# Weight sums of block products made in DRAM by accumulating transfers, five plain pairs, and block products kept in the program's order

## The chip, the cores and the metric

The kernel runs on one core of a Trainium2 chip. Its time is the device time of one execution in microseconds. TensorE (PE) multiplies matrices out of SBUF into PSUM, VectorE (DVE) and ScalarE (ACT) work elementwise, GpSimd (POOL) computes nothing here, and SyncE (SP) issues nearly all transfers. Each engine takes its instructions in a fixed order, which a planner sets when the program is built: it goes by the order in which the program was written, by estimated costs, and by when operands are due, and it may move an instruction ahead of an earlier one on its engine.

## What is computed

One step of a small backbone of two layers on 512 latent and 128 context tokens, D = 1024. Layer 0 has a bidirectional scan (SSD) as token mixer, layer 1 differential attention. After each mixer comes a ConvGLU network:

```python
def conv_ffn(h, up_w, conv_w, conv_b, down_w):
    u = dwconv(h @ up_w, conv_w, conv_b)      # up_w 1024 x 5632, width-3 filter along the tokens
    a, v = jnp.split(u, 2, axis=-1)
    return (jax.nn.silu(a) * v) @ down_w      # down_w 2816 x 1024
```

Every sublayer is preceded by an RMS norm with shift, scale and gate that are computed from a conditioning vector by a 1024 x 6144 matrix per layer (the "modulation").

## The kernel before

Activations lie transposed, channels on partitions, the 640 tokens along the free axis. For near-fp32 products each operand is split in two fp32r parts, `hi` (ScalarE copies with rounding) and `lo` (VectorE subtracts), and a product is three matmuls: hi·hi, hi·lo, lo·hi. One step of a plain product is a matmul of 256 and one of 384 columns.

The stages in order are SSD, first network, attention, second network. A network has 22 pairs of hidden tiles (a tile of `a`, a tile of `v`, 128 channels each) and goes through them in three groups; after each group the down projection adds what the group's tiles give (`project_out`, the last time `project_last`). A weight unit is a tile of 128 x 1024 floats (512 KB). SyncE loads it into one of four buffers (`prefetch`, L301), `cast` (L309) splits it into one of five pairs of hi and lo buffers, and `nextw` (L332) hands it over, loads up to three units ahead and casts one ahead. Up projections use PSUM tiles of two banks, of which there are three.

In the second network pairs 0 to 3 (`STD = 4`) are plain. From pair 4 on, the up projection works on blocks: the contraction (1024) is cut in two halves of 512, the tokens in two halves of 320, and the pair has two rows of weight blocks, x1 x2 for `a` and y1 y2 for `v`. A Strassen-Winograd scheme takes 7 block products, where the plain form would need 8; each has 4 contraction steps of 3 matmuls, so 12 matmuls of 320 columns. It needs sums of blocks of the activations (`sums`, L61, made once, while the first plain pairs run, by a task that `hook` advances; VectorE adds, ScalarE and VectorE split) and sums of blocks of the weights, per pair four (s1 to s4). These are made by VectorE in `stage` (L119), as `s[0] = y1 + y2`, `s[1] = s[0] - x1`, `s[2] = x1 - y1`, `s[3] = x2 - s[1]`, each 128 x 512, and every one of the seven blocks is split by itself, except that x1 and x2 share one wide split in every second pair. `plan` (L102) writes the order of the products by hand, `stage` works up to `LOOK = 7` products ahead of it.

A pair's products go 1, 2, (3 of the pair before), 6, (4 of the pair before), 5, 7 (`pair`, L175). Products 1, 6, 7 and 4 go into one PSUM half tile: 6, 7 and 4 add to what is there, and before each of them ScalarE copies the state so far out (`ua`, `uv`), since it is part of a result. VectorE adds products 2, 3 and 5 to these copies. Product 3 adds to 5's bank. Three half tiles serve a pair and six alternate. Then `epilogue` filters `a` and `v` along the tokens (ScalarE and VectorE), takes the SiLU, multiplies, and splits the result for the down projection. Products 3 and 4 of the last pair of a group come in the down projection behind its first tile (`between`, L210).

During the first network a task, `mod_rest` (L703), computes the modulation of layer 1 on VectorE: 48 columns, each from a 512 KB load on SP's queue (`mw`, two buffers) and two reductions (L725).

Of the kernel before, what the change touches and what calls it, by code (L numbers as in the profile page):

```python
# [41 lines left out]
STD = 4  # L42
HT = T // 2
LOOK = 7
# [5 lines left out]
class Blocks:  # L50


    def __init__(self, st, h, epilogue, pool):
        self.st, self.h, self.epilogue, self.pool = st, h, epilogue, pool
        self.ops = {}
        self.pend = None
        self.spare = None
        self.half = None
        self.units = sorted(st.paired)

    def sums(self):  # L61
# [5 lines left out]
        for j in range(4):  # L67
# [34 lines left out]
    def plan(self, p0, p1):  # L102

        self.seq, self.done, self.at = [], 0, 0
        for p in range(p0, p1):
            prev = p > p0
            self.seq += [(1, p), (2, p)] + [(3, p - 1)] * prev + [(6, p)] + [(4, p - 1)] * prev + [(5, p), (7, p)]
        self.seq += [(0, p1 - 1), (3, p1 - 1), (4, p1 - 1)]

    def place(self):  # L110

        if self.half is None:
            hi, lo = self.st.parts()
            self.half = hi[:, 512:], lo[:, 512:]
            return hi[:, :512], lo[:, :512]
        o, self.half = self.half, None
        return o

    def stage(self, upto):  # L119

        st = self.st
        k1, k2 = slice(0, 512), slice(512, 1024)
        while self.done < min(upto, len(self.seq)):
            i, p = self.seq[self.done]
            self.done += 1
            if i == 0:
                self.half = None
                st.cast(self.units[2 * (p - STD)] + 2)
                continue
            o = self.ops.setdefault(p, {})  # L130
            if i == 1:
                u = self.units[2 * (p - STD)]
                st.prefetch(u + 1)
                x, y = st.wraw[u], st.wraw[u + 1]
                s = [self.pool.tile([P, 512], F32, tag=f"s{n}", name=f"s{n}_{p}", bufs=1) for n in range(1, 5)]
                st.tt(s[0], y[:, k1], y[:, k2], ALU.add)
                st.tt(s[1], s[0], x[:, k1], ALU.subtract)
                st.tt(s[2], x[:, k1], y[:, k1], ALU.subtract)
                o["raw"] = {1: x[:, k1], 2: x[:, k2], 4: y[:, k2], 5: s[0], 6: s[1], 7: s[2], 3: s[3]}
                if self.half is None:  # L140
                    hi, lo = st.parts()
                    st.split_w(hi, lo, x)
                    o[1], o[2] = ((hi[:, k], lo[:, k]) for k in (k1, k2))
            if i == 6:
                st.tt(o["raw"][3], o["raw"][2], o["raw"][6], ALU.subtract)
            if i not in o:
                o[i] = self.place()
                st.split_w(*o[i], o["raw"][i])

    B = {1: "11", 2: "21", 3: "22", 4: 4, 5: 1, 6: 2, 7: 3}  # L150
# [24 lines left out]
    def pair(self, p):  # L175
        st = self.st
        st.wi = self.units[2 * (p - STD)] + 2
        st.prefetch(st.wi + 1)
# [31 lines left out]
    def between(self, i, p0, p1):  # L210

        st = self.st
# [9 lines left out]
        if i == 6:  # L222
            self.stage(LOOK)


class Step:


    def __init__(self, ctx, tc, a):
# [12 lines left out]
        self.paired = set()  # L242
        self.npart = 0
# [57 lines left out]
    def prefetch(self, upto):  # L301
        while len(self.wraw) <= min(upto, len(self.units) - 1):
            u = len(self.wraw)
            ap, n = self.units[u]
            r = self.pw.tile([P, 1024], F32, tag="raw", name=f"raw{u}", bufs=RAW)
            self.nc.sync.dma_start(r[:, :n], ap)
            self.wraw[u] = r

    def cast(self, upto):  # L309
        while len(self.wcast) <= min(upto, len(self.units) - 1):  # L310
            u = len(self.wcast)
            self.prefetch(u)
            if u in self.paired:
                self.wcast[u] = None
                continue
            n = self.units[u][1]
            hi, lo = (t[:, :n] for t in self.parts())
            self.split_w(hi, lo, self.wraw[u][:, :n])
            self.wcast[u] = hi, lo

    def parts(self):
        v = self.npart
        self.npart += 1
        wp, t, b = (self.pw, "w", 3) if self.px is None or v % 5 < 3 else (self.px, "x", 2)
        return [wp.tile([P, 1024], F32R, tag=t + nm, name=f"w{nm}{v}", bufs=b) for nm in ("hi", "lo")]

    def split_w(self, hi, lo, raw):

        self.act(hi, raw, AF.Copy)
        self.tt(lo, raw, hi.bitcast(F32), ALU.subtract)  # L330
# [136 lines left out]
    def project_out(self, h, ks, g, tiles=range(KT), after=None):  # L467

        for i in tiles:
            ps = self.dense_ps("po")  # L470
            self.dense(ps, self.nextw(), ks, h)
# [231 lines left out]
    def mod_rest(self, l, t0, pool):  # L703
# [11 lines left out]
        for t in range(t0 - 1, 48):  # L715
# [8 lines left out]
            for c in range(2):  # L724
                nc.vector.tensor_tensor_reduce(w if c else junk, w, cb[:, c, :], 1.0, 0.0, ALU.mult, ALU.add,  # L725
                                               self.mod[l][:, t, c:c + 1])
                yield 2 if self.down else 7
            if t % KT == KT - 1:
# [16 lines left out]
    def ffn(self, l, h, nextnorm, pool):  # L745
# [27 lines left out]

        self.start_tiles(h)
        done = 0
        sub = SUB[l]
        blk = Blocks(self, h, epilogue, pool) if l else None
        for s, (k0, k1) in enumerate(sub):
# [3 lines left out]
            if blk and s == 0:  # L782
                blk.plan(STD, end)
# [14 lines left out]
            after = blk and (lambda i: blk.between(i, done, min(sub[s + 1][1] + 1, FT) if not last else done))  # L798
            if not last:
                self.project_out(mid, range(k0, k1), self.gate(l, 1), after=after)  # L800
            else:
                self.project_last(mid, range(k0, k1), self.gate(l, 1), nextnorm, parts="CD" if l else "AB",
                                  after=after)
# [550 lines left out]
    def weight_units(self):  # L1354
        a = self.a
        u = [(a["w_dt"], 512)]
# [3 lines left out]
        u += [(a["w_in"][j], 1024) for j in order]  # L1360
        for hf in range(2):
            u += [(a["w_so"][i, :, hf * 1024:(hf + 1) * 1024], 1024) for i in range(KT)]

        def ffn(l):
            done = 0
            out = []
            for k0, k1 in SUB[l]:
                while done < min(k1 + 1, FT):
                    if l and done >= STD:
                        self.paired |= {len(u) + len(out), len(u) + len(out) + 1}  # L1370
                    out.extend([(a["w_up"][l, done], 1024), (a["w_up"][l, FT + done], 1024)])
                    done += 1
                out.extend([(a["w_dn"][l, i, :, k0 * P:k1 * P], (k1 - k0) * P) for i in range(KT)])
# [3 lines left out]
        for hd in range(8):  # L1377
            u += [(a["w_qkv"][8 * j + hd], 1024) for j in range(3)]
# [137 lines left out]
```

## Time and profile before

| | |
|---|---|
| median of 3 runs (lowest to highest) | 1885.05 us (1882.87 to 1887.03) |
| the profiled execution | 1884.19 us |
| its span, first to last instruction | 1882.4 us |
| granted TensorE clock, mean | 0.991 |
| busy: PE, DVE, ACT, POOL | 98%, 79%, 53%, 0% |
| read from and written to HBM | 201.63 MB, 5.96 MB |

All times below are microseconds from the start of this execution's span. TensorE works on the first network from about 568 to 1038, on attention to about 1406, on the second network from then on: its first block product begins at 1465.6, its last down projection ends near 1867. "PE" rows are matmuls, "PEld" rows the loading of stationary operands, and "<-" in brackets names what ended an engine's idle time before a row. L277, L280, L283 and L286 are helpers, so rows of theirs are told apart by their tiles: `whi`, `wlo` are weight parts, `s` the four sums, `ba`, `bb`, `bc` the PSUM tiles of block products, `up` and `po` those of plain up and down projections, `T` and `h11` activation parts.

### The profile page before, as it was taken

The numbers are of one execution on the slowest core, as the hardware profiler recorded it, in microseconds if no ns is written. First come the engines' busy times: TensorE is split into PE (matmuls) and PEld (weight loads), VectorE is DVE, ScalarE is ACT, GpSimd is POOL, SyncE is SP. The second block draws the span as 40 slices with busy tenths as digits, with TensorE's granted clock in tenths as the row PEclk, the third lists the DMA queues.
The fourth block names the chain that finished last, engine by engine and source line by source line (L and its number), as shares of the span: only waits on it lengthen the run. The fifth ranks groups of instructions, "written<-read, shape, count | busy, mean of one in ns | idle before, by whom it ended". The sixth has DMA issues, their size and how long they took to land. (4 is left out here: it accounts for less than half of the span.)

```text
span 1882.4 us, 32863 instructions
## 1 busy us (share of the span) xinstructions
PE 1841.4 (98%) x13117; PEld 1727.3 (92%) x13117; DVE 1478.4 (79%) x2886; ACT 991.6 (53%) x1880; POOL 0.2 (0%) x4
## 2 busy tenths in 40 slices
PE   7999999999999999999999999999999899999997
PEld 4789899989989999999999988888899799999996
DVE  4689999999748999984455877778779885975974
ACT  2479687879336441442343565656546442643651
POOL 0000000000000000000000000000000000000000
PEclk9999999999999999999999999999999899999998
DMA  9735243446543556632222212111031131231221
GB/s 344 256 109 147 92 133 117 117 136 177 186 136 108 190 182 218 188 119 80 77 68 68 88 52 64 47 59 40 23 119 52 55 104 60 73 114 57 68 79 56
DMA packets 79521, 209.72 MB, mean 111 GB/s; under 512 B 9116, under 2 KB 15880, under 8 KB 79240
## 3 DMA queue, kind: packets, MB, share of 16 engines
q1 hardware_dynamic: 78792, 207.10, 34.7%
q8 instruction: 103, 1.69, 0.4%
q10 hardware_dynamic: 576, 0.52, 0.1%
q14 instruction: 50, 0.41, 0.1%
HBM read 201.63 MB, written 5.96 MB: 110 GB/s over the span
## 5 line engine op out<-in xcount | busy, mean ns | idle before, releaser
L277 ACT ACTIVATE whi<-raw 128x1024 fp32r<-128x1024 f32 (+4 forms) x238 | 228.3, 961 | 303.1 <-PE po L286 187.7
L283 DVE TENSOR_TENSOR wlo<-raw,whi 128x1024 fp32r<-128x1024 f32 (+4 forms) x238 | 261.9, 1102 | 79.7 <-ACT whi L277 67.8
L280 DVE SCALAR_TENSOR_TENSOR xr<-po,mod,xr 128x256 f32<-128x256 f32 (+2 forms) x231 | 89.3, 434 | 138.0 <-PE po L286 137.9
L286 PE MATMUL po<-ml,whi 128*128 128x256 f32 (+1 forms) x704 | 168.2, 310 | 0.0
L286 PE MATMUL po<-mh,whi 128*128 128x256 f32 (+1 forms) x704 | 168.0, 310 | 0.0
L286 PE MATMUL po<-mh,wlo 128*128 128x256 f32 (+1 forms) x704 | 167.8, 310 | 0.0
L286 PE MATMUL up<-h01h,wlo 128*128 128x256 f32 (+1 forms) x656 | 149.4, 308 | 0.0
L286 PE MATMUL up<-h01l,whi 128*128 128x256 f32 (+1 forms) x656 | 149.3, 308 | 0.0
L286 PE MATMUL up<-h01h,whi 128*128 128x256 f32 (+1 forms) x656 | 149.3, 308 | 0.0
L286 PEld LDWEIGHTS po<-mh,whi 128*128 128x128 f32 x704 | 128.4, 188 | 0.5 <-ACT mh L277 0.2
L286 PEld LDWEIGHTS po<-mh,wlo 128*128 128x128 f32 x704 | 128.8, 188 | 0.0
L286 PEld LDWEIGHTS po<-ml,whi 128*128 128x128 f32 x704 | 128.6, 188 | 0.1
L286 PEld LDWEIGHTS up<-h01h,wlo 128*128 128x128 f32 x656 | 119.3, 188 | 0.0
L286 PEld LDWEIGHTS up<-h01l,whi 128*128 128x128 f32 x656 | 119.3, 188 | 0.0
L286 PEld LDWEIGHTS up<-h01h,whi 128*128 128x128 f32 x656 | 119.2, 188 | 0.0
L277 ACT ACTIVATE whi<-s 128x512 fp32r<-128x512 f32 x72 | 44.5, 626 | 60.7 <-PE po L286 20.6
L277 ACT ACTIVATE mh<-cv 128x640 fp32r<-128x640 f32 x44 | 32.5, 738 | 79.3 <-DVE cv L283 79.1
L277 ACT ACTIVATE e<-sl,sm 128x640 f32<-128x640 f32 x64 | 50.4, 790 | 40.2 <-DVE sm L1225 39.8
L286 PE MATMUL z<-h00h,whi 128*128 128x256 f32 (+1 forms) x256 | 62.9, 325 | 0.0
L277 ACT ACTIVATE e<-rb,Ctok 128x128 f32<-128x128 f32 x160 | 56.4, 390 | 12.3 <-issue 10.0
L277 ACT ACTIVATE ca<-ca 128x640 f32<-128x640 f32 x44 | 32.4, 736 | 57.0 <-DVE ca L280 56.8
L286 PE MATMUL z<-h00l,whi 128*128 128x256 f32 (+1 forms) x256 | 59.8, 312 | 0.0
(558 smaller groups left out, 5154.7 us busy)
## 6 DMA issues: line engine op xcount, KB each, us to landing
raw<-in_w_up SPq DMA_DIRECT2D x88, 512.0 KB, 3.4
mw<-in_modT SPq DMA_DIRECT2D x48, 512.0 KB, 3.6
raw<-in_w_in SPq DMA_DIRECT2D x40, 512.0 KB, 5.2
rb<-rowd SPq DMA_DIRECT2D x40, 512.0 KB, 5.3
raw<-in_w_dn SPq DMA_DIRECT2D x32, 448.0 KB, 3.4
raw<-in_w_qkv SPq DMA_DIRECT2D x24, 512.0 KB, 3.4
mr<-in_mod SPq DMA_DIRECT2D x44, 256.0 KB, 5.5
raw<-in_w_so SPq DMA_DIRECT2D x16, 512.0 KB, 4.2
```

The costliest lines, as they stand in the source:

```text
L277: return self.nc.scalar.activation(out, in_, func, **k)
L280: return self.nc.vector.scalar_tensor_tensor(out, in0, s, in1, op0, op1)
L283: return self.nc.vector.tensor_tensor(out, a, b, op)
L286: return self.nc.tensor.matmul(out, lhsT, rhs, start=start, stop=stop, **k)
```

## The change

- `STD` goes from 4 to 5: pairs 0 to 4 are plain, 17 pairs work on blocks.
- The four weight sums of these 17 pairs are made in DRAM. `weight_sums` issues, on GpSimd's queue, four plain copies and four transfers that add to what lies at their destination (`accum_op`), each for up to three pairs at once and 256 KB a pair. Each waits for those whose result it uses. They are issued in six groups of nine transfers from within `mod_rest`, at columns 4, 12, 20, 28, 36 and 44; a first transfer of two floats, which reads the modulation column just made, ties the group to that time. VectorE and SP have no part in it.
- So that only additions are needed, `v`'s block row is taken with the opposite sign: the activation sums change theirs, operand 2's parts are made negated (`neg`), and the three filter taps of `v` in the block pairs are multiplied by -1 once, at the start of the second network.
- The blocks then are ordinary weight units, loaded by SP from the weights or from the sums in the order in which the products use them: one wide unit for products 1 and 2 where these fall together, otherwise two halves of 256 KB in one buffer. One `cast` splits a unit of 128 x 1024. `plan`, `place`, `stage` and their lists go, and so do the buffers s1 to s4.
- In the second network's weights the two contraction halves of a tile lie apart in DRAM (`w_blk`), so a plain unit is loaded in rows of 2 KB rather than 4.
- `nextw` casts three units ahead (`AHEAD`) for block products and the second network's down projections, and loads up to five ahead, still into four buffers.
- The first matmul of each block product is pinned behind everything that was traced on TensorE before it (`keep_in_program_order`). Other matmuls are not pinned.

```diff
-STD = 4
+STD = 5
-LOOK = 7
+AHEAD = 3
...
-            st.tt(t1, a[:, c2], a[:, c1], ALU.subtract)
-            st.tt(t2, b[:, c2], t1, ALU.subtract)
-            st.tt(t4, b[:, c1], t2, ALU.subtract)
+            st.tt(t1, a[:, c1], a[:, c2], ALU.subtract)
+            st.tt(t2, b[:, c2], t1, ALU.add)
+            st.tt(t4, t2, b[:, c1], ALU.subtract)
...
-                st.split_w(t[:, c1], t[:, c2], x)
+                st.split_w(t[:, c1], t[:, c2], x, i == 2)
...
     def finish_sums(self):
         st, h, t = self.st, self.h, self.t
-        self.stage(LOOK)
+        st.cast(st.wi + 1)
...
     def product(self, ps, i, p):
         st = self.st
-        self.at += 1
-        self.stage(self.at + LOOK)
-        wh, wl = self.ops[p].pop(i)
+        if self.half is None:
+            hi, lo = st.nextw(AHEAD)
+            wh, wl = hi[:, :512], lo[:, :512]
+            if hi.shape[1] > 512:
+                self.half = hi[:, 512:], lo[:, 512:]
+        else:
+            (wh, wl), self.half = self.half, None
...
-                st.mm(ps, a[:, c], b, not acc and j == 0 and m == 0, j == 3 and m == 2, skip_group_check=acc)
+                x = st.mm(ps, a[:, c], b, not acc and j == 0 and m == 0, j == 3 and m == 2, skip_group_check=acc)
+                if j == 0 and m == 0:
+                    st.tc.keep_in_program_order(x)
...
-    def between(self, i, p0, p1):
-
-        st = self.st
+    def between(self, i):
         if i == 0:
+            self.half = None
             self.third()
             self.fourth()
             self.half = self.spare = None
-            if p1 > p0:
-                self.plan(p0, p1)
-        if i == 4:
-            st.cast(st.wi + 2)
-            self.stage(4)
-        if i == 6:
-            self.stage(LOOK)
...
-    def nextw(self):
+    def nextw(self, ahead=1):
         u = self.wi
         self.wi += 1
-        self.prefetch(u + 3)
-        self.cast(u + 1)
+        self.prefetch(u + 2 + ahead)
+        self.cast(u + ahead)
         return self.wcast[u]
...
+            if t % 8 == 4 and t < 48:
+                n = -(-(FT - STD) // 6)
+                p0 = STD + t // 8 * n
+                if p0 < FT:
+                    self.weight_sums(p0, min(p0 + n, FT), self.mod[l][0:1, t, :])
...
+            t = cw[:, FT + STD:, 0:3]
+            nc.vector.tensor_scalar(t, t, -1.0, None, ALU.mult)
...
+            def piece(i, p):
+                if i in (1, 2, 4):
+                    return a["w_blk"][p + FT * (i == 4), int(i > 1)], 512
+                return (lambda: self.wsum[p - STD, (5, 6, 7, 3).index(i)]), 512
...
+                    if seq[n][0] == 1:
+                        out.append(up(seq[n][1])[0])
+                    else:
+                        out.append([piece(*q) for q in seq[n:n + 2]])
+                    n += 2
...
+    def weight_sums(self, p0, p1, mark):
+
+        g, w, s = self.nc.gpsimd, self.a["w_blk"], self.wsum
+        rows = lambda x: x.rearrange("n p c -> n (p c)").rearrange("n (r c) -> r n c", c=2048)
+        a1, a2, n = slice(p0, p1), slice(FT + p0, FT + p1), slice(p0 - STD, p1 - STD)
+        put = lambda i, x, **k: g.dma_start(rows(s[n, i]), rows(x), **k)
+        add = dict(accum_op=ALU.add)
+        g.dma_start(s[p0 - STD, 0, 0:1, 0:2], mark)
+        put(0, w[a2, 0])
+        put(2, w[a1, 0])
+        put(0, w[a2, 1], **add)
+        put(2, w[a2, 0], **add)
+        put(1, s[n, 0])
+        put(1, w[a1, 0], **add)
+        put(3, s[n, 1])
+        put(3, w[a1, 1], **add)
```

More of the change, by code (lines that the diff above doesn't have):

```diff
@@ L58, in __init__ @@
         self.half = None
-        self.units = sorted(st.paired)
     def sums(self):
@@ L119, in stage @@
-    def stage(self, upto):
-        st = self.st
[L122 to L143, printed above, removed]
-            if i == 6:
[L145 to L148, printed above, removed]
@@ L797, in ffn @@
                 self.drain(self.modtask)
-            after = blk and (lambda i: blk.between(i, done, min(sub[s + 1][1] + 1, FT) if not last else done))
             if not last:
-                self.project_out(mid, range(k0, k1), self.gate(l, 1), after=after)
+                self.project_out(mid, range(k0, k1), self.gate(l, 1), after=blk and blk.between)
             else:
                 self.project_last(mid, range(k0, k1), self.gate(l, 1), nextnorm, parts="CD" if l else "AB",
-                                  after=after)
+                                  after=blk and blk.between)
     def ssd_consts(self, pool):
@@ L1367, in ffn @@
             for k0, k1 in SUB[l]:
[L1368 to L1371, printed above, removed]
+                end = min(k1 + 1, FT)
+                while done < end and not (l and done >= STD):
+                    out += up(done)
                     done += 1
-                out.extend([(a["w_dn"][l, i, :, k0 * P:k1 * P], (k1 - k0) * P) for i in range(KT)])
+                seq = []
+                for p in range(done, end):
+                    prev = p > done
+                    seq += [(1, p), (2, p)] + [(3, p - 1)] * prev + [(6, p)] + [(4, p - 1)] * prev + [(5, p), (7, p)]
+                n = 0
+                while n < len(seq):
+                    if seq[n][0] == 1:
+                        out.append(up(seq[n][1])[0])
+                    else:
+                        out.append([piece(*q) for q in seq[n:n + 2]])
+                    n += 2
+                dn = down(k0, k1)
+                if seq:
+                    dn.insert(1, [piece(3, end - 1), piece(4, end - 1)])
+                done = end
+                out += dn
             return out
```

86 lines of the change are left out of this document (36 added, 50 removed).

## The prediction

> **What bounds the kernel now.** I read the page first, then the windows view by stage, the waits of the one stretch that loses time, its timeline, the groups by form, and the transfers.
>
> ```profile
> span 1882.4 us, 32863 instructions
> PE 1841.4 (98%) x13117; PEld 1727.3 (92%) x13117; DVE 1478.4 (79%) x2886; ACT 991.6 (53%) x1880; POOL 0.2 (0%) x4
> PEclk9999999999999999999999999999999899999998
> ```
>
> TensorE is busy 98% of the span, so a gain has to come from TensorE waits or from fewer TensorE cycles. The clock line shows one dip inside the program, slice 32 of 47 us each, which begins at 1459 us. The windows view cuts that place out; its columns are length, then busy time of PE, PEld, DVE, ACT, POOL, then granted clock, DMA share and GB/s.
>
> ```profile
> 575.00:700.00 125.00, 125.00 (x849) 125.00 (x848) 120.29 (x219) 66.84 (x90) 0.00 (x0) 1.00 0.53 169
> 700.00:755.00 55.00, 55.00 (x377) 55.00 (x377) 54.12 (x98) 9.26 (x10) 0.00 (x0) 1.00 0.68 215
> 1405.00:1465.00 60.00, 60.00 (x433) 59.16 (x432) 55.48 (x123) 39.77 (x68) 0.00 (x0) 1.00 0.14 45
> 1465.56:1489.80 24.24, 17.19 (x74) 14.93 (x73) 21.05 (x38) 8.27 (x15) 0.00 (x0) 0.72 0.20 66
> 1489.80:1527.20 37.40, 36.71 (x242) 35.64 (x243) 31.85 (x59) 22.85 (x39) 0.00 (x0) 1.00 0.31 89
> 1600.00:1720.00 120.00, 119.39 (x805) 1.00 0.27 82
> ```
>
> The first network (575 on) and the plain pairs of the second (1405 to 1465) leave TensorE no gap. The first 24 us of block products do: 74 matmuls at a granted clock of 0.72. After 1490 almost nothing is lost (119.39 of 120 us busy). So the change can win in one place, the start of the block products. Its waits (total us, times, longest) and parts of its timeline:
>
> ```profile
> ACT whi L277 <- PE ba L286: 9.0, 2, 6.8
> PE ba L286 <- DVE ua L283: 2.1, 1, 2.1
> PE ba L286 <- DVE wlo L283: 1.8, 1, 1.8
> PE ba L286 <- ACT ua L277: 1.7, 2, 1.2
> ```
>
> ```profile
> 1461.74 0.46 PE L286 MATMUL up<-h11h,wlo 128*128 128x256 f32 x2
> 1464.68 0.46 PE L286 MATMUL up<-h11h,whi 128*128 128x256 f32 x2
> ...
> 1469.17 0.42 PE L286 MATMUL ba<-h11h,wlo 128*128 128x320 f32 x1 [1.84 <-DVE wlo L283]
> 1471.49 0.47 PE L286 MATMUL ba<-h11h,wlo 128*128 128x320 f32 x1
> 1471.99 0.44 ACT L277 ACTIVATE ua<-ba 128x320 f32<-128x320 f32 x1 [3.25 <-PE ba L286]
> 1472.48 0.63 PE L286 MATMUL ba<-h11h,whi 128*128 128x320 f32 x1 [0.53 <-ACT ua L277]
> 1473.18 0.47 PE L286 MATMUL ba<-h11h,wlo 128*128 128x320 f32 x1
> 1475.32 0.47 PE L286 MATMUL ba<-h11l,whi 128*128 128x320 f32 x1
> 1478.36 0.31 PE L286 MATMUL bc<-h11h,whi 128*128 128x320 f32 x1
> 1479.39 0.31 PE L286 MATMUL bc<-h11l,whi 128*128 128x320 f32 x1
> ```
>
> Cadences from the starts: a plain step (one 256 and one 384 column matmul) takes (1464.68 - 1461.74)/10 = 0.294 us. A block matmul of 320 columns takes (1479.39 - 1478.36)/7 = 0.147 us, and (1475.32 - 1473.18)/8 = 0.268 us while the clock is down. VectorE is late with weight parts and sums (21.05 of 24.24 us busy, after 55.48 of 60), TensorE waits 1.84 us for one, loses its clock and computes six microseconds at little over half speed; then ScalarE and VectorE are late once more. Of the 74 matmuls two belong to the plain pair; 72 x 0.147 = 10.6 us were needed, 24.24 were taken: **13.6 us lost**, some 7 by waits and the rest by the clock.
>
> The Trainium skill, "TensorE: Matmul & The Clock Gate", section "What's actually happening", has the clock halve after an idle window of about 3.4 us. Here no single wait was that long (1.84 us, 0.47 us before it) and the clock fell all the same, so the row decides; by the rule a stall left over of 1 or 2 us would cost itself alone.
>
> **The change part by part.**
>
> *Sums and weight parts on VectorE.* Groups by form, 1465 to 1815 us:
>
> ```profile
> L283 DVE TENSOR_TENSOR wlo<-s,whi 128x512 fp32r<-128x512 f32 x72 | 48.7, 687 | 9.6 <-ACT whi L277 9.6
> L283 DVE TENSOR_TENSOR wlo<-raw,whi 128x512 fp32r<-128x512 f32 x34 | 23.1, 689 | 0.2
> L283 DVE TENSOR_TENSOR wlo<-raw,whi 128x1024 fp32r<-128x1024 f32 x14 | 17.1, 1223 | 2.6 <-ACT whi L277 2.6
> L283 DVE TENSOR_TENSOR s<-raw,s 128x512 f32<-128x512 f32 x18 | 12.4, 688 | 0.1
> L283 DVE TENSOR_TENSOR s<-raw,raw 128x512 f32<-128x512 f32 x18 | 12.4, 688 | 0.0
> L283 DVE TENSOR_TENSOR s<-s,raw 128x512 f32<-128x512 f32 x17 | 11.7, 688 | 0.1
> L283 DVE TENSOR_TENSOR s<-raw 128x512 f32<-128x512 f32 x17 | 11.7, 686 | 0.0
> L277 ACT ACTIVATE whi<-raw 128x1024 fp32r<-128x1024 f32 x14 | 14.8, 1055 | 18.2 <-PE po L286 10.7 <-PE ba L286 7.3 <-PE bb L286 0.3
> ```
>
> Four sums of 0.69 us a pair go: 72 x 0.688 = 49.5 us of VectorE. The parts are then made 1024 wide: 3.5 a pair at 1.223 = 4.3 us, against five of 0.688 and half a wide one, two halves of 0.69 in the other pairs, 4.7 us. A pair asks VectorE for 3.2 us less of the 7 x 12 x 0.147 = 12.3 us that TensorE takes for it. By itself that is hidden work, except at the start, where it is what TensorE waits for.
>
> *Five plain pairs.* Pair 4 becomes 48 x 0.294 = 14.1 us in place of 12.3: **+1.8 us** on the path. In return VectorE gets 14 us more before the first block product. The four pairs up to 1465, with the norm's tail and the activation sums, kept it busy 55.48 us, 13.9 a pair; the added pair has neither norm nor sums, only an epilogue and weight parts, and the block sums that stood in the queue at 1465 are gone, so what it is behind can be caught up. The first block unit is then an ordinary unit, cast ahead. So nearly all of the 13.6 us goes: **-13.6**, and I leave **+1.0** for what is still late (bounds 0 and 7, the waits without the clock). What is late next is an epilogue of the plain pairs, wanted only by the down projection three block pairs (37 us) on.
>
> *Products in the program's order.* Each product's first matmul is put behind all that was traced on TensorE. Where a run of blocks begins, 6 follows 1 with only product 2 between, and 7 follows 6 with only 5 between, both into a bank that ScalarE must copy first. The cover is 12 x 0.147 = 1.76 us. The chain in the timeline, from the issue of the last matmul (1471.49) to the first that may write the bank again (1472.48), takes 1.0 us with a free ScalarE, so 0.76 us is left; a wide cast in the way (1.055 us) overruns it by 0.3. Behind a waiting product stand all later ones, then their copies on ScalarE and adds on VectorE. Three runs x two places x 0.2: **+1.2 us** (bounds 0 and 6 x 0.6 = 3.7). In later pairs two products or more lie between, 3.5 us of cover: I take 0 (bounds -2, the small switches after 1490, and the second rival).
>
> *Weights by pieces.* 17 pairs ask for 119 blocks of 256 KB: 31.2 MB where 17.8 were loaded, in 10 wide and 99 half transfers where 34 were; at 0.33 us of SP each that is 25 us more over 400. 1.84 MB in 12.3 us is 149 GB/s; the windows show 215 GB/s moved at 700 to 755 with no TensorE gap. A buffer comes free four units (14 us) before its data is due and a load lands in 3.4 us. At nothing; without that cover each unit could lose up to 3.4 us.
>
> *The sums in DRAM.* 17 x 8 transfers of 0.262 MB = 35.7 MB written, 54 issues on POOL (it has 4 instructions now; nothing stands behind them). Each group starts when a modulation column (4, 12, ... 44) is done, so somewhat behind the loads of these columns, and is wanted from about 1475: from 616 on, 41 GB/s would do. They run beside these:
>
> ```profile
> raw<-in_w_up SPq DMA_DIRECT2D x88, 512.0 KB, 3.4
> mw<-in_modT SPq DMA_DIRECT2D x48, 512.0 KB, 3.6
> L718 SPq DMA_DIRECT2D mw<-in_modT x48: 327/328/328, 584.9 to 815.6; - x48
> ...
> DVE junk L725 <- DMA mw<-in_modT: 1.3, 3, 0.8
> ...
> 717.48 3.13 SPq L718 DMA_DIRECT2D mw<-in_modT  x2
> ...
> 722.35 1.22 DVE L725 CUSTOM_DVE_ANT_0 junk<-mw,cbc 128x1024 bf16<-128x1024 f32 x1
> ...
> ACT whi L277 <- PE po L286: 96.5, 21, 6.1
> ```
>
> A share of 0.68 at 215 GB/s means 316 GB/s at full use; 35.7 MB then take 113 us of all engines, 169 if the four accumulating transfers in eight read twice. Were all of it laid on the loads of 585 to 900 us, 48 of the modulation and 45 of weights (one each 7.05 us), each would land 1.8 us later. A modulation load has 722.35 - 717.48 = 4.9 us for its 3.6, so some would hold VectorE 0.5 us, and VectorE has no room there (54.12 of 55). TensorE would not feel it soon: casts wait for TensorE to free a buffer (96.5 us of such waits), not the other way. **+0.3 us** (bounds 0 and the third rival). No row has an accumulating transfer; the nearest are the plain loads, and I stay near them since only the total matters.
>
> The sign change of the filter taps is one small VectorE operation; its data are issued at 1368.8, 35 us ahead of the start of that network:
>
> ```profile
> L748 SPq DMA_DIRECT2D fcw<-in_fcw x2: 327/328/328, 535.4 to 1368.8; - x2
> ```
>
> **Sum:** -13.6 + 1.0 + 1.8 + 1.2 + 0.3 = **-9.3 us**. The profiled execution took 1884.19 us (span 1882.4 and 1.8 around it), the median of the runs is 0.86 above: 1885.05 - 9.3 = **1875.7 us**. Measurements of this kernel tell 0.2%, 3.8 us, from no change.
>
> **Rivals.** *First, half of the loss stays.* VectorE was 92% busy before the start and still is in pairs 0 to 3; if it is as late after pair 4, the 7 us of waits stay and only the clock's share goes: -6.6 + 1.8 + 1.2 + 0.3 = -3.3, 1881.8. For it: the activation sums are not made smaller. Against: 14 us of new room.
>
> *Second, slower: the order itself costs.* Now the planner puts a later product into each wait; pinned, products 6 and 7 of every pair wait for ScalarE's copy, which stands behind whatever ScalarE does. One such wait later on:
>
> ```profile
> 1646.41 0.41 PE L286 MATMUL bb<-h11h,whi 128*128 128x320 f32 x1 [0.61 <-ACT ua L277]
> ```
>
> At 0.61 us each, 34 products lose 20.7 us in place of 1.2: 1895. It decides from 10.5/34 = 0.31 us each. For it: ScalarE is in order and waits up to 6.8 us at a cast. Against: ScalarE loses 14 us of narrow casts, is busy little over half, and 3.5 us of cover beat a chain of 1.0.
>
> *Third, the sums crowd the first network.* If modulation loads take twice as long, 7.2 us, two columns need 7.2 + 2.6 = 9.8 us of a down unit of 8 x 3 x 0.294 = 7.05: VectorE falls back 22 us in eight units, and behind its gate additions TensorE has three PSUM tiles, two units or 14 us, of cover. 8 us come through: 1884; with no cover, 1898.
>
> The Trainium skill, "DMA: Bandwidth & Descriptors", section "Issuing engines are not separate DMA queues", speaks for this rival: transfers of SP and GpSimd share the same 16 engines and interleave. This trace has no transfer from POOL, so it can't show how far they slow each other.
>
> *Fourth, the sums are late* (under 41 GB/s) and TensorE waits at 1475 for them: tens of microseconds. Against it stand 650 us between the last modulation load and the first use.
>
> **Numbers.** Forecast (1869 to 1880) 0.62, first rival 0.14, second 0.12, third 0.10, fourth 0.02. Faster by over 0.2% (below 1881.3): the forecast, a third of the first and a little of the third, 0.68. Within: most of the first and half the third, 0.15. Slower: the second, fourth and the rest, 0.17. The low end is all 13.6 us and the small switches gone with nothing given back but the plain pair, 1885 - 13.6 - 2 + 1.8 = 1871, and 3 us below it for what I can't see; the high end takes the first and third rival and the beginning of the second, 1888.
>
> **What would show it.** Right: at the start of the block products, then near 1479, TensorE without gaps over 1 us and the clock at 1.00; no sums on VectorE; the first network's windows still full; waits for a copy only at the first pair of a run. Wrong: a clock under 1 there, waits of products 6 and 7 for ScalarE in every pair, idle VectorE before the modulation columns, or block products that wait for a weight transfer.

## The result and the profile after

The changed kernel takes **1936.05 us** (median of 4 runs, 1932.70 to 1938.54) beside 1885.74 us for the kernel before, measured with it (1882.87 to 1887.03): a ratio of 1.0268, 95% interval 1.0248 to 1.0288. It is 2.7% slower, where 0.5% faster was forecast. Its profiled execution has a span of 1934.0 us, 51.6 more than before.

The page of the kernel after: span, busy time, and from the 40 slices (48 us each) those of the clock and of the DMA engines.

```profile
span 1934.0 us, 32975 instructions
PE 1847.1 (96%) x13129; PEld 1731.5 (90%) x13129; DVE 1433.1 (74%) x2759; ACT 984.1 (51%) x1825; POOL 38.7 (2%) x58
...
PEclk8999999999999999999999999999999999999998
DMA  9944334345542788897422212111131333333321
```

TensorE's busy time grew by 6 us, the rest of the 51.6 is idle time. VectorE was relieved of 45 us. The dip of the clock in slice 32 is gone, and there is a new one in the first. The transfers have a new hill in slices 14 to 19.

Cutting both spans at TensorE's first matmul of each stage tells where the time went (us; each row is one profiled execution):

| kernel | SSD | first network | attention | plain pairs | blocks and down tiles | tail | span |
|---|---|---|---|---|---|---|---|
| before | 568.5 | 469.5 | 368.9 | 58.7 | 401.2 | 15.7 | 1882.4 |
| after | 588.9 | 483.4 | 366.5 | 72.8 | 406.4 | 16.1 | 1934.0 |
| difference | +20.4 | +13.9 | -2.4 | +14.1 | +5.2 | +0.4 | +51.6 |

Kernels that leave the SSD stage and attention as they were have 566 to 570 and 367 to 371 there, so differences of some 4 us in these two columns say nothing. Three losses are to be explained: +20 in a stage that the change was not meant to touch, +14 in the first network, and block products that take 5 us more although one pair fewer of them is left.

**The SSD stage.** POOL's timeline in the kernel after (start, duration, what came before it in brackets):

```profile
1.27 1.25 POOL L1365 DMA_DIRECT2D wsum<-in_w_blk  x2 [0.83 <-POOLq L1498]
10.53 0.90 POOL L1365 DMA_DIRECT2D wsum<-in_w_blk  x1 [8.00 <-issue]
...
77.71 0.87 POOL L1365 DMA_DIRECT2D wsum<-in_w_blk  x1 [8.82 <-issue]
```

Twelve transfers of the sums, 9 MB, run from 1.27 us on. Only sum 0 of a group has the small transfer that ties it to a modulation column. The first copy into sum 2 and the addition behind it read weights alone and wait for nothing that the kernel computes, and the planner put them first, for all six groups. The windows view, first of the kernel before and then after (length, busy time of PE, PEld, DVE, ACT, POOL, granted clock, DMA share, GB/s):

```profile
0.00:50.00 50.00, 39.44 (x423) 25.39 (x424) 22.86 (x53) 14.87 (x27) 0.20 (x4) 1.00 0.96 341
50.00:100.00 50.00, 48.40 (x348) 40.57 (x347) 33.36 (x59) 23.60 (x43) 0.00 (x0) 1.00 0.74 243
760.00:860.00 100.00, 100.00 (x682) 100.00 (x681) 86.41 (x150) 46.02 (x57) 0.00 (x0) 1.00 0.45 139
860.00:925.00 65.00, 65.00 (x443) 65.00 (x442) 25.57 (x44) 15.46 (x17) 0.00 (x0) 1.00 0.25 82
```

```profile
0.00:50.00 50.00, 26.09 (x252) 13.50 (x253) 15.96 (x33) 10.56 (x16) 5.54 (x12) 0.86 0.99 334
50.00:100.00 50.00, 44.77 (x391) 36.17 (x389) 31.97 (x61) 18.48 (x30) 3.57 (x5) 0.97 1.03 349
760.00:860.00 100.00, 93.43 (x620) 91.86 (x619) 85.21 (x149) 28.06 (x34) 9.91 (x14) 0.98 0.89 262
860.00:925.00 65.00, 62.65 (x413) 62.38 (x413) 41.22 (x70) 25.02 (x31) 7.82 (x11) 0.97 0.76 206
```

The first 50 us were the one stretch where the transfer engines were already nearly full (0.96). With the sums among them TensorE does 252 matmuls there instead of 423. It now waits for transfers: directly for rows of the modulation (`modrow`), where the kernel before had no such wait of its matmuls, and 9.4 instead of 6.8 us for a ScalarE that itself waits for loads of `x`. Its waits from 0 to 100 us, after (total us, times, longest):

```profile
PE ms L230 <- ACT sq L221: 9.4, 1, 9.4
PE modrow L230 <- DMA mp1x<-in_modp: 5.8, 3, 2.7
PE modrow L230 <- DMA mp<-in_modp: 4.3, 2, 3.0
```

**The first network.** The lower two rows of the windows show 6.6 + 2.4 us of idle TensorE between 760 and 925. Its 1033 matmuls there also take some 4.6 us longer than at the pace before (93.43 us for 620 against 100 us for 682, and so on), at a granted clock of 0.98 and 0.97. Waits in the first network, and the transfers (KB each, us from issue to landing), after:

```profile
DVE junk L669 <- DMA mw<-in_modT: 22.7, 12, 3.3
...
PE up L230 <- DVE xr L224: 4.5, 2, 2.5
PE up L230 <- ACT uraw L221: 4.4, 3, 2.4
```

```profile
mw<-in_modT SPq DMA_DIRECT2D x48, 512.0 KB, 5.5
wsum<-in_w_blk POOLq DMA_DIRECT2D x30, 768.0 KB, 8.1
```

A modulation load lands in 5.5 us instead of 3.6. VectorE, in order, waits 22.7 us for these loads instead of 1.3, and its gate additions (`xr`), which free PSUM tiles, stand behind the waiting reductions. ScalarE in turn waits for VectorE, up to 22.8 us at one filter, and its copies of up tiles (`uraw`), which free PSUM tiles too, stand behind that.

**The block products.** TensorE's waits from 1455 to 1850 us, after:

```profile
PE bb L230 <- DVE uv L227: 13.9, 7, 2.7
PE ba L230 <- ACT ua L221: 6.8, 10, 1.0
PE bb L230 <- DVE ua L227: 4.1, 7, 0.6
PE ba L230 <- DVE ua L227: 2.2, 3, 0.9
```

27 us in 27 waits, none for a weight part or a transfer: all for copies and additions that read a PSUM tile. Two of them in the timeline, after:

```profile
1630.49 0.31 PE L230 MATMUL ba<-h11h,wlo 128*128 128x320 f32 x1
1630.84 0.44 ACT L221 ACTIVATE ua<-ba 128x320 f32<-128x320 f32 x1 [0.52 <-PE ba L230]
1631.33 0.42 PE L230 MATMUL ba<-h11h,whi 128*128 128x320 f32 x1 [0.53 <-ACT ua L221]
...
1640.58 1.94 DVE L224 SCALAR_TENSOR_TENSOR cv<-uv,fcw,cv 128x511 f32<-128x511 f32 x4 [0.55 <-ACT cv L221]
1641.85 0.31 PE L230 MATMUL ba<-h11h,wlo 128*128 128x320 f32 x1
1642.43 1.22 DVE L227 TENSOR_TENSOR wlo<-raw,whi 128x1024 fp32r<-128x1024 f32 x1
1643.57 0.82 DVE L227 TENSOR_TENSOR cv<-ca,cv 128x640 f32<-128x640 f32 x1
1644.30 0.48 DVE L227 TENSOR_TENSOR uv<-uv,bb 128x320 f32<-128x320 f32 x1
1644.84 0.42 PE L230 MATMUL bb<-h11h,whi 128*128 128x320 f32 x1 [2.68 <-DVE uv L227]
```

The first is product 2 behind product 1. Product 2 writes the second bank of the two-bank tile `ba`; product 1's result lies in the first. No datum passes between them, and still 2 waits until ScalarE has copied 1 out. The second is product 1 of the next pair: it writes the second bank of `bb`, whose first bank holds product 5 of the pair before, and waits for VectorE's `uv<-uv,bb`, which is queued behind a filter, a weight part and a product. So a matmul waits until the *other half* of its tile has been read. All 27 waits are of this kind: ten are product 2 behind 1, seven are product 1 of the next pair behind `uv`, and ten are product 6 behind the addition (`ua`) that reads product 3 or, at the start of a run of blocks, product 2.

### The profile page after: what moved, and what is told of

It reads as the page before. It is cut to its first block, busy times and chain, and to the rows that moved or that the text cites. A ratio compares the mean times of both kernels' runs of the same rounds, so it can differ in the third digit from the quotient of the medians.

```text
span 1934.0 us, 32975 instructions
## 1 busy us (share of the span) xinstructions
PE 1847.1 (96%) x13129; PEld 1731.5 (90%) x13129; DVE 1433.1 (74%) x2759; ACT 984.1 (51%) x1825; POOL 38.7 (2%) x58
## 3 DMA queue, kind: packets, MB, share of 16 engines
q1 hardware_dynamic: 92152, 220.47, 34.7%
q0 software_dynamic: 5312, 35.66, 7.6%
## 4 chain that ended last, share of the span: by engine, by line
PE 77%; DVE 10%; DMA 9%; ACT 2%; issue 1%; SPq 0%; DVEq 0%; ACTq 0%
PE po L230 22%; PE up L230 10%; PE z L230 6%; PE st L230 5%; PE bc L230 5%; PE bb L230 4%; PE x L230 4%; DMA mw<-in_modT 4%; PE ba L230 4%; PE yp L230 3%; PE v L230 3%; PE q L230 2%; PE k L230 2%; PE sl L230 2%; DVE junk L669 2%; PE ov L230 2%
## 5 line engine op out<-in xcount | busy, mean ns | idle before, releaser
L221 ACT ACTIVATE whi<-raw 128x1024 fp32r<-128x1024 f32 (+4 forms) x257 | 261.7, 1019 | 357.9 <-PE po L230 215.6
L227 DVE TENSOR_TENSOR wlo<-raw,whi 128x1024 fp32r<-128x1024 f32 (+4 forms) x257 | 301.8, 1175 | 126.6 <-ACT whi L221 114.9
L669 DVE CUSTOM_DVE_ANT_0 junk<-mw,cbc 128x1024 bf16<-128x1024 f32 x48 | 58.6, 1221 | 22.9 <-DMA mw<-in_modT 22.7
```

The lines of the kernel that those rows point to most:

```text
L221: return self.nc.scalar.activation(out, in_, func, **k)
L227: return self.nc.vector.tensor_tensor(out, a, b, op)
```

## The experiments

**Set 1: the three losses apart.** The first run takes out the pins and nothing else, the second ties the copies that ran at the start.

```diff
 (after, without the pins)
-                x = st.mm(ps, a[:, c], b, ...)
-                if j == 0 and m == 0:
-                    st.tc.keep_in_program_order(x)
+                st.mm(ps, a[:, c], b, ...)
```

> The changed kernel without the pin on each block product's first matmul; all else stays. Theory (three separate losses: about 20 us at the start by sums that nothing ties to the first network, about 14 us in the first network by modulation loads that land late, about 20 us in the second network by the pinned order): only the third goes. The second network, 495 us from its first matmul to the end, falls to about 466 us (475.6 of before, less the 13.6 us at the start of its block products, plus 1.8 for the plain pair and a little); total about 1907 us. Rival (the second network loses by its weight pieces, 149 GB/s in place of 85, or by transfers from the sums): it stays at 495 us, total 1936 us.

Measured: 1905.53 us, ratio 1.0115 (1.0092 to 1.0138). The second network takes 72.8 + 375.7 + 16.9 = 465.4 us instead of 495.3. The pins cost 29.9 us. That is the 27.0 us of waits less the 1.8 us that are left without pins, and three stretches of some 3.5 us at a granted clock of 0.51 to 0.55, each behind a wait of 2.7 us, which cost about 1.5 us apiece (an estimate: 12 matmuls at 0.27 us instead of 0.147). Weight pieces and sums read from DRAM are all still in this kernel, and its second network is 10.2 us shorter than that of the kernel before: the rival fell. Its first network, in which nothing was changed, took 477.2 us here and not 483.4: VectorE waited 19.8 us for modulation loads of 4.8 us, and 7.7 us came through. So the size of that loss varies, at least from 8 to 14 us.

```diff
 (after, sum 2 tied as well)
         g.dma_start(s[p0 - STD, 0, 0:1, 0:2], mark)
+        g.dma_start(s[p0 - STD, 2, 0:1, 0:2], mark)
```

> The changed kernel with a second transfer of two floats per group, from the same modulation column into sum 2, so that this sum's copy and addition can't be issued before that column either. Theory: the start is the kernel before's again (first network from 568 in place of 589 us), and the first network, which gets these 9 MB as well, loses some 4 us more than now; total about 1920 us. Rival (the 35.7 MB cost what they cost wherever they run): 1936 us, the 20 us come back in the first network. Pins and the second network as in the changed kernel (495 us).

Measured: 1917.97 us, ratio 1.0197 (1.0160 to 1.0233). The SSD stage is back at 566.1 us; the first network, which now has all the sums, goes to 487.1. The start is explained by the untied transfers.

**Set 2: is the first network just the wrong place?** All groups are tied to the keys of the first six attention heads, where the mean DMA share was about 0.2 before; once with the pins and once without.

```diff
 (after: the six groups leave mod_rest and go here; sum 2 tied too)
             k, kp = self.att_evac(self.next_tile(h, "k"), hd, "k", pool)
+            n = -(-(FT - STD) // 6)
+            p0 = STD + hd * n
+            if p0 < FT:
+                self.weight_sums(p0, min(p0 + n, FT), kp[0:1, 0:2])
```

> The changed kernel with all sums, both ties included, issued in attention: a group for each of the first six heads, tied to that head's keys instead of a modulation column. Theory: start and first network as in the kernel before (568 us, 469 us), attention at 0.20 of the transfer engines hides the sums; the second network stays 495 us by its pins: total about 1902 us. Rival (the sums slow any stage they lie in): attention grows from 367 by 10 to 20 us, total 1912 to 1922 us.

> Sums in attention and no pins, the rest of the change kept. Theory: the three losses are separate and add, so what is left is the forecast of the prediction less its term for the order: about 1874 us, under the kernel before by 11 us. Rival (the losses overlap, or the block products lose by pieces too): 1885 us or more.

Measured: 1921.81 us, ratio 1.0205 (1.0188 to 1.0222), and without pins 1893.21 us, 1.0054 (1.0037 to 1.0071). The first network is back at 469.5 in both, but attention goes from 369 to 386.2 and 390.1. My theory (harmless where the transfers have room) fell. Waits from 1036 us to the end of attention in the kernel with pins:

```profile
PE wt L1233 <- ACT wpT L221: 9.6, 4, 3.6
...
DVE o L224 <- DMA rbc<-rsd: 13.6, 5, 4.2
```

Attention sends the row factors of a norm to DRAM and loads them back spread over all partitions (`rbc`). VectorE's next operation needs them. One such load before, and one with the sums beside it:

```profile
1305.96 0.33 SPq L402 DMA_DIRECT2D rbc<-rsd  x1
1309.37 0.88 DVE L280 SCALAR_TENSOR_TENSOR o<-o,sg,rbc 128x640 f32<-128x640 f32 x1
```

```profile
1276.22 0.33 SPq L346 DMA_DIRECT2D rbc<-rsd  x1
1283.69 0.88 DVE L224 SCALAR_TENSOR_TENSOR o<-o,sg,rbc 128x640 f32<-128x640 f32 x1 [3.87 <-DMA rbc<-rsd]
```

At most 3.4 us from issue to use before, with no wait; 7.5 with the sums. The store ahead of the load (`rsd`) is slower too: 1.6 us lie between the two issues before, 2.2 here and up to 5.0 with the sums. VectorE stands still, the factors for `w` come late, and TensorE waits at the transposes `wt`. The DMA share of this stretch (last but one number), sums included, was only 0.70:

```profile
1228.00:1325.00 97.00, 88.26 (x560) 76.11 (x558) 66.14 (x132) 50.70 (x108) 13.81 (x20) 0.95 0.70 172
```

So a free share of the engines is no cover for a load that an in-order engine is about to need.

**Set 3: halves, pins and the place of the sums.** First, the late sums and the pins are kept, but every half product and every half down tile gets a PSUM tile of one bank; there are six (`psh`), the same space as before, from the end of the plain pairs on. `Two` lets a down tile of two such halves be used as one. Products and down tiles change together in all the kernels with one-bank tiles; what each brings was not separated.

```diff
 (late sums and pins, one-bank tiles)
-        return self.psd.tile([P, 1024], F32, tag="d", name=name)
+        if self.psh:
+            return Two(self.half(name), self.half(name))
+        return self.psd.tile([P, 1024], F32, tag="d", name=name)
+    def half(self, name):
+        return self.psh.tile([P, 512], F32, tag="h", name=name)
...
     def banks(self):
         st = self.st
-        if self.spare is None:
-            x, y = st.dense_ps("ba"), st.dense_ps("bb")
...
+        return [st.half(n)[:, :HT] for n in ("ba", "bb", "bc")]
```

> As the kernel with all sums in the attention stage and the pinned order, but each half product of the blocks, and each half of a down tile, gets a one-bank accumulator tile of its own. Theory of halves (a pinned product waits because the other half of its two-bank tile is still to be read): the stretch of blocks and down tiles falls from 406 us to 376 us, as without pins, and the time from 1921.8 to 1892 us. Rival (the pinned order leaves TensorE nothing to fill a wait with, whatever tile the product writes): the stretch stays over 395 us, 1911 us or more.

Measured: 1883.73 us, ratio 1.0009 (0.9997 to 1.0020). Blocks and down tiles take 368.3 us, 38 less than with two-bank tiles and the same pins, 8 less than expected; the plain pairs, at whose end the tiles are exchanged, take 74.4 instead of 72.8. Of all waits of TensorE's matmuls from 1455 to 1850 us one is left:

```profile
PE ba L236 <- ACT uraw L227: 1.4, 1, 1.4
```

That settles what the pins did: with a tile for each half the order is harmless, the sharing of a tile was the cost. The pins only took away the planner's means to work around it. In an unpinned kernel (the spread one below) the planner cuts a product in two to fill the gap:

```profile
1641.25 0.31 PE L228 MATMUL ba<-h11h,wlo 128*128 128x320 f32 x1
1641.40 0.45 PE L228 MATMUL bb<-T,whi 128*128 128x320 f32 x2
...
1642.08 0.41 PE L228 MATMUL ba<-h11h,whi 128*128 128x320 f32 x1
```

Between the end of one product in `ba` and the start of the next one there, four matmuls of another are slipped in (two of them in the rows left out).

The Trainium skill, "PSUM — Partial Sum Buffer", section "PSUM bank collisions raise a hardware error", says that accesses of two engines have to be kept apart within one bank and one group of 32 partitions; different banks may be used at once. The waits here are between different banks, so they are more than that rule asks for. That the waits are set by tile when the program is built follows from these runs; which step of the building does it is not shown.

Then the kernel before with pins, and the kernel before with a fifth plain pair:

```diff
 (before, pinned)
-                st.mm(ps, a[:, c], b, ...)
+                x = st.mm(ps, a[:, c], b, ...)
+                if j == 0 and m == 0:
+                    st.tc.keep_in_program_order(x)
 (before, five plain pairs)
-STD = 4
+STD = 5
```

> The kernel before with the pins alone: the first matmul of each block product keeps the program's order; four plain pairs, sums on VectorE. Theory of halves: the same waits appear here, the second network goes from 475.6 us to 495-505 us and the time to 1905-1915 us. Rival (the pins cost only beside the new sums and weight pieces): the second network stays under 482 us, under 1893 us.

> The kernel before with five plain pairs in place of four and nothing else. Theory (VectorE is late at the start of the blocks because it makes the sums of the weights there): the 13.6 us stay, the extra plain pair costs its 1.8 us, 1885-1889 us. Rival (the plain pair gives VectorE the time that it lacks, and the gain at the start belongs to the pair and not to the sums): 1872-1877 us.

Measured: with pins 1912.02 us, ratio 1.0155 (1.0140 to 1.0171), the second network at 504.7 instead of 475.6; the pins cost 29 us in either kernel. With five pairs 1878.87 us, 0.9977 (0.9966 to 0.9987). That lies between the two theories: the plain pairs take 14.1 us more, the blocks 19.9 less, so the extra pair alone takes 5.8 us off these two stretches.

Last, no pins, two-bank tiles, and the sums where no engine on the path waits for a small load: two groups behind the last modulation column, four in the second network.

```diff
 (after, unpinned, sum 2 tied, sums spread)
+            if t == 47:
+                for i in (0, 1):
+                    self.sum_group(i, self.mod[l][0:1, t, :])
...
         def epilogue(p, ua, uv):
+            if l and p < 4:
+                self.sum_group(p + 2, ua[0:1, 0:2])
```

> No pins, both untied copies tied, and the six groups of sums moved to stretches in which nothing on the path waits for a small load: two behind the last modulation column of the first network (from 824 us), four behind the copies of the first four plain pairs of the second network. Theory (the sums cost time only where they delay a load that another engine is waiting for): start 566, first network 470, attention 369, second network 449 us and 16.5 behind it, the span ends at 1870 us, 1870-1875 us in time. Rival (36 MB more through the DMA engines cost some 17-20 us in any stage): 1885 us or more.

Measured: 1875.29 us, ratio 0.9952 (0.9940 to 0.9965), a span of 1870.1 with 567.4, 469.5, 366.9 and 466.4. The same 36 MB now cost nothing that these runs can tell: from 1500 to 1550 us TensorE is busy 50.00 of 50 us beside a DMA share of 0.84, more than the 0.70 above. The load that held VectorE up is harmless again:

```profile
L222 DVE SCALAR_TENSOR_TENSOR o<-o,sg,rbc 128x640 f32<-128x640 f32 x7 | 6.2, 881 | 0.0
```

(busy, mean ns, idle before it). This is the kernel that the forecast of 1875.7 us described, without the pins.

**Set 4: what is each part worth?** Both cures together, the same without pins, and the kernel before with five pairs and one-bank tiles, with all sums of weights still made on VectorE.

```diff
 (after: sums spread as above, pins kept, one-bank tiles; then the same without pins)
+        return [st.half(n)[:, :HT] for n in ("ba", "bb", "bc")]
 (before: five plain pairs, one-bank tiles)
-STD = 4
+STD = 5
+        return [st.half(n)[:, :HT] for n in ("ba", "bb", "bc")]
```

> Both cures together: sums in the two quiet stretches, the pinned order kept, each half product in its own one-bank tile. From the stages measured so far: start 567.4, first network 469.5, attention 367, plain pairs 74.4, blocks and down tiles 368.3, 16.9 behind: 1863.5 us of span, 1864-1870 us in time. If the sums delay the blocks' own weight loads now that they run beside the second network, the stretch of blocks grows by what is lost, 1872 us or more.

> The same without the pins. Theory of halves: with one bank per half product the order costs and brings nothing, within 3 us of the kernel with the pins (1864-1870 us). Rival (the fixed order itself brings the 7 us by which split tiles beat the unpinned kernel): 1871-1877 us.

> The kernel before with five plain pairs and one-bank tiles, all sums of weights on VectorE as before. It asks what the sums in DRAM are worth by themselves: if VectorE is still late for the blocks, 3-6 us above the kernel with the sums in DRAM and the same tiles, 1869-1874 us; if five pairs and the tiles already take all there is, the same time as that kernel, 1864-1869 us.

Measured, with before at 1883.85 us: 1867.30 us, ratio 0.9917 (0.9903 to 0.9931); 1867.39 us, 0.9917 (0.9903 to 0.9930); 1866.60 us, 0.9913 (0.9900 to 0.9927). The three can't be told apart. With one bank per half product the order neither costs nor brings anything, and the sums in DRAM bring nothing either.

```diff
 (before: one-bank tiles alone)
 STD = 4
...
+        return [st.half(n)[:, :HT] for n in ("ba", "bb", "bc")]
```

> The kernel before with one-bank tiles alone: four plain pairs, sums on VectorE. With five pairs as well it took 0.9913 of before. If the fifth plain pair is needed for VectorE's lateness at the start of the blocks, the 4-6 us that it brought by itself are missing: 1870-1874 us beside a before of 1884. If the tiles alone bring it all: 1868 us or less.

Measured: 1868.78 us beside a before of 1883.50, ratio 0.9917 (0.9904 to 0.9931). The time lies between the two cases of the expectation (1868 and 1870), but the ratio equals that of the full versions, so the fifth pair brings nothing beyond the 2.5 us or so that these intervals can tell. TensorE's waits from 1455 to 1850 us, and the first 25 us of the block products, in this kernel:

```profile
PE ba L292 <- DVE wlo L289: 1.6, 3, 0.7
PE ba L292 <- ACT uraw L283: 1.0, 1, 1.0
```

```profile
1468.00:1493.00 25.00, 23.23 (x152) 22.32 (x153) 25.00 (x46) 14.60 (x27) 0.00 (x0) 1.00 0.25 83
```

152 matmuls at a clock of 1.00, where the kernel before did 74 in 24 us at 0.72, with VectorE busy all of the time: it still makes every sum. VectorE is still late here, which costs the 1.6 us for `wlo`; what is gone are the waits for the other half of a tile and the fall of the clock. Why the clock held through these shorter waits was not tested. The second network takes 60.0 + 382.3 + 16.5 = 458.8 us instead of 475.6. A change of PSUM tiles alone beats the kernel before by 0.8%, and the changed kernel by more; nothing that was tried beside it adds to that.

## Why the prediction was wrong

The forecast was -9.3 us. Measured, from the stages and the runs: +20.4 (start), +13.9 (first network), +29.9 (pins), -2.4 (attention, no more than its scatter), and 465.4 - 475.6 = -10.2 for the rest of the second network; together 51.6.

- *The sums in DRAM, +0.3 us: failed, in two ways.* "Each group starts when a modulation column (4, 12, ... 44) is done" was wrong. The tie holds only for what touches sum 0, and the copies into sum 2 were free to start at 1.27 us; I had read the issue order and not asked which transfer depends on the tie. That is the +20.4. And "only the total matters" was wrong: it spread 35.7 MB over a bandwidth, 1.8 us per load as the worst case, while a modulation load went from 3.6 to 5.5 us just where VectorE had no room. The third rival came true in its mechanism and nearly in its size: VectorE was to fall back 22 us and waited 22.7, of which 13.9 came through instead of 8, and 7.7 in the kernel without pins. The closeness is partly luck: the rival had loads of 7.2 us, and they took 5.5. Its chance of 0.10 was too low, since the same row that spoke for it (VectorE busy 54.12 of 55 us) stood in the forecast's own step. In attention the sums cost 13 to 21 us (386.2, 390.1 and, in the first kernel with one-bank tiles, 382.4 us instead of 368.9) at a lower share of the engines, where VectorE had to wait for a small load on the path; in the quiet stretches, nothing.

  The Trainium skill, "DMA: Bandwidth & Descriptors", section "Queues, rings and completion order", says that a DMA engine takes one packet of each queue in turn. On the profile's page of the kernel after, POOL's queue has 35.66 MB in 5312 packets, 6.7 KB each, SP's 220.47 MB in 92152, 2.4 KB each. Whether these are packets in the sense of that rule is not shown, and no run varied their size, so how the sums lengthen the loads stays open; that they do is shown by the kernels that have the sums elsewhere, where a modulation load lands in 3.5 or 3.6 us.
- *The pinned order, +1.2 us: failed.* "In later pairs two products or more lie between, 3.5 us of cover: I take 0" counted the distance between products of the same half. The wait is by tile, and the other half of the tile was written or read by the product just before. That put 27 waits of 27.0 us in all into the rows in place of 1.2; the pins cost 29.9 us by the run without them, 29 by the pinned kernel before. The evidence stood in the quoted timeline: the matmul at 1472.48 that waits 0.53 us for `ua` is product 2, which has no use for the copy of product 1; I took it for product 6. The second rival had the order as a cost of 20.7 us, by waits at the copies in every pair, but saw them at products 6 and 7, as true needs behind a busy ScalarE. None of the 27 is at product 7, none is a need of the datum, and three quarters of the time (20.2 of 27.0 us) are waits for VectorE.
- *The start of the block products, -13.6 us: right in size, its cause misread in part.* Without pins, blocks and down tiles go from 401.2 to 375.7; less the 84 x 0.147 = 12.35 us of the pair that became plain, that is 13.2 gained, and the clock stays at 1.00. But the forecast put the loss on VectorE, "late with weight parts and sums". With VectorE's work unchanged, one-bank tiles end nearly all of it too. The forecast's own list of waits said so: the 2.1 us and 0.5 of the 1.7 us for `ua` are for the other half of a tile, 1.8 are for a weight part; the other 1.2 us are product 7, which adds to the bank being copied and has to wait. The extra pair by itself brought 7.5 of the 13.2 (401.2 - 381.3 - 12.35), which is 5.8 net of what it costs; how the rest divides between the lighter VectorE and the planner's other order was not measured.
- *The plain pair, +1.8 us: right.* The plain pairs took 58.7 and take 72.8 us, 14.1 for the fifth, against 12.35 for the block pair that it replaces.
- *Weight pieces, 0: right.* TensorE has no wait for a transfer or a weight part in the pinned blocks; in the unpinned kernel the stretch with the same pieces takes 375.7 us.
- *The first rival* (half of the loss stays) and *the fourth* (sums late) did not show.

## What to carry to other kernels

In these kernels a wait was set by the tile, not by the datum. When two results that live at different times share a tile, each may wait for the other's readers, and a planner that reorders can hide much of this until the order is fixed; ask of each wait whether the waiting instruction needs that datum at all, and give it a tile of its own first. Work moved to the transfers is free only in stretches where no in-order engine waits for a load, so look for the small loads on the path and not at the mean share, and check for every transfer of a group that something ties it to its time.

## What the runs showed of the hardware that was not expected

- Transfers on POOL's queue lengthened the loads of SP's queue well short of full use: from 3.6 to 5.5 us (median) for the 512 KB modulation loads at a DMA share of 0.82 to 0.89, and from at most 3.4 to 7.5 us, from issue to use, for one load of the row factors at 0.70.
- A DRAM to DRAM transfer of 768 KB from the weights (copies and additions together) took 8.1 us to land in the kernel after, where a load of 512 KB beside it took 5.5.
- The granted clock fell after waits well under 3 us, but not after all of them. In the pinned blocks of the kernel after, three of the four waits of 2.7 us were followed by some 3.5 us at about half clock (0.51 from 1674.0 to 1677.5 us), and one was not (1.00 from 1644.8 to 1648.0). In the kernel before, waits of 0.5 and 1.8 us close together, which left TensorE busy for 0.69 of the 3.0 us from 1466.2 to 1469.2, were followed by 6 us at half clock (0.50 from 1469.6 to 1475.9). What decides it was not tried.
